# Handing out a projection's products in halves beside a windowed attention, each half bound to an attention unit's scores or to another unit's output

## The chip, the core and the metric

The kernel runs on one core of a Trainium2 chip, all in float32, with products of two parts each (below). The metric is the device time of one execution in microseconds (us). Times of several executions are given by their median.

## The reference, cut to what matters

```python
h = rms_norm(x, norm_mix)                     # x: 2048 tokens x 1024
z = h @ w_in                                  # q_A k_A v_A q_B k_B v_B gate_A gate_B
yA = windowed_gqa(q_A, k_A, v_A, sink)        # |t-s| <= 128, ALiBi, a sink logit per head
yB = neighborhood_attn(q_B, k_B, v_B, rpb)    # 8 x 16 places of a 32 x 64 grid
x = x + (sigmoid(gA) * (yA @ Wp_A) + sigmoid(gB) * (yB @ Wp_B)) @ W_out
x = x + relu(rms_norm(x, norm_mlp) @ W_up) ** 2 @ W_down
out = rms_norm(x, norm_final)
```

There are 8 query heads over 2 key heads in A, 8 heads in B, and 64 features per head.

## The kernel before, in words

TensorE does every product in three passes: each float32 operand is split into a high part and a rest, and the high-by-high, high-by-rest and rest-by-high products are added up in one PSUM bank (`mm3`, L203 to L205). The rest of the program is arranged so that TensorE is always given something to do.

The input projection is done for the first 1024 tokens in one stage of its own. For the other 1024 tokens (two blocks of 512, `b` 2 and 3) its products are **filler**: they are handed out while the two attentions run. One filler product is `feature_tile` (L207): 8 chunks of the 1024 features by three passes, 24 matmuls of 128x512 into one of the two banks called `mm`. When the 24 are done, ScalarE and VectorE read the bank and write the result in two parts (`z`), and SyncE sends it to memory. A column tile of 128 features is two such products. `qk_tile` (L706) and `v_tile` (L719) make them: load the weights, split them (`whl`), then product and eviction for block 2, then the same for block 3. The first 12 column tiles (24 products, 576 matmuls) belong beside attention A; gate tiles follow them beside attention B.

Attention A is 32 **units** (`attn_a`, L771), one for a key head and 128 queries. A unit has two parts, with a `yield` between them. The first makes four score products (L792, two matmuls each into one of three banks `s`); VectorE adds the bias and takes the maximum (L794), ScalarE the exponentials (L799), VectorE sum and reciprocal (L800, L801), and GpSimd the scaling (L803). The second turns the shares by TensorE, three or two times four transposes into one of two banks `pt` (L810), has ScalarE copy (L813) and VectorE subtract (L814) to get their two parts `ph` and `pl`, multiplies both with v (L815, L816, bank `av`), and adds the two halves of that bank (L821 on ScalarE, L822 on VectorE).

`drive` (L836) writes the units so that the second part of unit k comes behind the first part of unit k+2. This is done in two calls: 14 units, then 18.

The order on each engine isn't the order of the source. A scheduler sorts each engine's instructions: the attention, which is written first, goes first wherever it is ready by the scheduler's own clock, and filler, which is written behind it, is put where the attention isn't ready. What keeps filler from being used up too early is `paced` (L846): piece n of the filler may stand on TensorE only behind an instruction kept in the list `done`. Such a bond orders the queue when the program is built; on the chip nothing waits for it. Before the change `done` holds one mark per unit, the last matmul with v (L816, appended in L817), and a piece is one whole product: piece n stands behind unit n*32/24 - 3 (rounded down), the first three behind nothing.

```python
def paced(filler, pieces, total, lag):
    for n in pieces:
        at = min(n * 32 // total - lag, 31)
        with tc.issue_after(done[at]) if at >= 0 else nullcontext():
            next(filler, None)
```

In the profile's names, `mm<-hT,whl` is filler, `s<-ka,qa` scores, `pt<-ident,sa` transposes, `av<-ph,va` and `av<-pl,va` the products with v.

Of the kernel before, what the change touches and what calls it, by code (L numbers as in the profile page):

```python
# [22 lines left out]
P = 128  # L23
KC = D // P
# [10 lines left out]
O_QA, O_KA, O_VA, O_QB, O_KB, O_VB, O_GA, O_GB = 0, 512, 640, 768, 1280, 1792, 2304, 3328  # L35
# [60 lines left out]
def encoder_layer(ctx, tc, x, norm_mix, w_in, b_gate, sink, rpb, w_pa, w_pb, w_out,  # L96
                  norm_mlp, w_up, w_down, norm_final, dist_a, mask_b, out):
    nc = tc.nc
    V, A, G, PE, SY = nc.vector, nc.scalar, nc.gpsimd, nc.tensor, nc.sync
# [99 lines left out]
    def cols(w, c, n=P):  # L199
        return w[:, c : c + n]  # L200

    def mm3(ps, lh, ll, rh, rl, first, last):
        PE.matmul(ps, lh, rh, start=first, stop=False)  # L203
        PE.matmul(ps, lh, rl, start=False, stop=False)  # L204
        PE.matmul(ps, ll, rh, start=False, stop=last)  # L205
# [371 lines left out]
    for p in range(2):  # L577
        t = T(xp, [P, D], F32, "xin", 8).rearrange("p (k c) -> p k c", k=4)
# [15 lines left out]
    for k in range(KC):  # L594
        ps = zbank(*tbanks[k % 6])
# [7 lines left out]
        else:  # L603
            h, l = (t[:, kk] for t in right[3])
# [41 lines left out]
    for q in range(2, len(QUADS)):  # L646
# [10 lines left out]
        if q in (5, 6):  # L657

            b = q - 3
# [24 lines left out]
    hp = {}  # L684
# [18 lines left out]
    h_pages(2)  # L703


    def qk_tile(col, scale, tiled=False):  # L706
        raw = load_slice([(cols(w_in[0], col), KC)])
        yield
        hl = split_slice(raw, V if col == O_KA else G)
        yield  # L710
        for b in (2, 3):
            ps = psum("mm", 2)
            feature_tile(ps, hl, hp[b])
            out = qk_parts(col, b, ps, T(wp, [P, 2, BT], F32, "z", 3))
            for dst, t in out:
                SY.dma_start(dst, t)
            yield

    def v_tile(col):  # L719
        raw = load_slice([(cols(w_in[0], col), KC)])  # L720
        yield
        hl = split_slice(raw, V if col == O_VA else G)
        yield
        for b in (2, 3):
            ps = psum("mm", 2)
            feature_tile(ps, hl, hp[b])
# [12 lines left out]
    for h in range(4):  # L739
        at = slice(h * A_Q, (h + 1) * A_Q)  # L740
# [10 lines left out]
    done, began, shares = [], [], []  # L751
# [19 lines left out]
    def attn_a(g, i):  # L771
# [11 lines left out]
        ka, v = kas[g], vas[g]  # L783
# [4 lines left out]
        for u, (lo, hi) in enumerate(span):  # L788
            n = hi - lo
            ps = psum("s", 3)  # L790
            for z in range(2):
                PE.matmul(ps[:, :n], q[:, u].rearrange("p h q -> p (h q)"), ka[:, z, base + lo : base + hi],  # L792
                          start=z == 0, stop=z == 1)
            V.tensor_tensor_reduce(out=s[:, u, lo:hi], in0=ps[:, :n], in1=bias_a[g][:, lo - u * A_Q : hi - u * A_Q],  # L794
                                   scale=1.0, scalar=sink_g, op0=ALU.add, op1=ALU.max, accum_out=mx[:, u : u + 1])
# [11 lines left out]
        for c in range(c0, c1):  # L807
# [8 lines left out]
            last = PE.matmul(po, v[:, i - 1 + c, :], pl, start=False, stop=c == c1 - 1).ins  # L816
        done.append(last)  # L817
        t = T(ap_, [64, 512], F32, "ya", 2)
# [24 lines left out]
        while last and live:  # L843
            next(live.pop(0), None)

    def paced(filler, pieces, total, lag):  # L846

        for n in pieces:
            at = min(n * 32 // total - lag, 31)
            with tc.issue_after(done[at]) if at >= 0 else nullcontext():  # L850
                next(filler, None)

# [11 lines left out]
            yield  # L864


    dense = [qk_tile(O_KA, 1.0), v_tile(O_VA)]
    dense += [qk_tile(O_QA + t * P, 0.125) for t in range(4)]
    for t in range(4):
        dense.append(qk_tile(O_KB + t * P, 0.125))  # L870
        dense.append(qk_tile(O_QB + t * P, 1.0, tiled=True))
        dense.append(v_tile(O_VB + t * P))
    dense += [gate_tile(f, (2, 3)) for f in range(16)]
    for n in (0, 0, 1):
        next(dense[n])
# [2 lines left out]
    fill = chain(dense)  # L878
# [182 lines left out]

    first_y = load_y(0)
    first_load = last_dma[0]
    paced(fill, range(20, 44), 38, 4)
    s_h.close()


# [297 lines left out]
    for b in range(NB):  # L1365
# [43 lines left out]
        for t in range(4):  # L1409
# [182 lines left out]
    for n in (1, 6, 2, 7, 5, 3, 4):  # L1592
        for group in ((range(8),) if n != 4 else (range(4), range(4, 8))):
# [14 lines left out]
            last = []  # L1608
# [55 lines left out]
```

## Time and profile before

| what | value |
|---|---|
| median of 3 executions | 2606.39 us (2603.34, 2606.39, 2606.54) |
| the profiled execution's own time | 2603.09 us |
| its span, first to last instruction | 2601.3 us |
| TensorE matmuls | busy 2570.3 us (99%), 12140 of them |
| VectorE, ScalarE, GpSimd busy | 1608.5 us, 1232.9 us, 366.8 us |
| first score product of attention A starts | about 363 us |
| last product with v of attention A starts | about 645 us |

A matmul's row in the profile gives its start and how long it took from there to its end. Matmuls overlap: the next one starts before the last has ended, so a row of 0.39 us may be followed by a start 0.23 us later. "Busy" is the time in which at least one is under way. What a matmul costs the queue is read from the distance of the starts.

### The profile page before, as it was taken

How to read it: one execution, taken by the hardware profiler on the slowest of the kernel's cores; microseconds unless marked ns; L12 is line 12 of the kernel's file. 1: busy time of each engine (PE TensorE's matmuls, PEld its weight loads, DVE VectorE, ACT ScalarE, POOL GpSimd, SP SyncE). 2: the span in 40 equal slices, each digit the busy share in tenths (PEclk: the TensorE clock that was granted, in tenths of full speed). 3: DMA queues.
4: the chain of work that ended last, by engine and by line, in shares of the span. 5: the costliest groups of instructions: out<-in, count | busy, mean ns of one | idle time of the engine just before them, and what ended most of it. 6: DMA issues, size and time to landing. Idle time of an engine off the chain costs nothing.

```text
span 2601.3 us, 34630 instructions
## 1 busy us (share of the span) xinstructions
PE 2570.3 (99%) x12140; PEld 2143.2 (82%) x12140; DVE 1608.5 (62%) x2621; ACT 1232.9 (47%) x2261; POOL 366.8 (14%) x493
## 2 busy tenths in 40 slices
PE   8999999999999999999999999999999999999999
PEld 6888788788888888888888888888888888888887
DVE  8866666665544444665478667766656534554766
ACT  5334356665655555542335544644454322323454
POOL 1000124444645531000000000100000000000010
PEclk9999999999999999999999999999999999999999
DMA  5657485465976746865466665844428825444555
GB/s 186 203 154 207 135 260 160 121 170 154 244 211 180 205 137 189 270 205 160 144 195 213 232 227 202 307 167 149 155 102 314 288 97 186 146 149 167 186 191 173
DMA packets 354128, 490.40 MB, mean 189 GB/s; under 512 B 28809, under 2 KB 188809, under 8 KB 351777
## 3 DMA queue, kind: packets, MB, share of 16 engines
q1 hardware_dynamic: 346896, 471.14, 57.2%
q10 hardware_dynamic: 7056, 17.04, 1.8%
q8 instruction: 96, 1.57, 0.3%
q14 instruction: 80, 0.65, 0.1%
HBM read 328.64 MB, written 159.45 MB: 188 GB/s over the span
## 4 chain that ended last, share of the span: by engine, by line
PE 92%; DVE 3%; DMA 2%; ACT 2%; issue 1%; SPq 0%; POOL 0%; POOLq 0%; ACTq 0%; DVEq 0%
PE b L302 16%; PE b L304 16%; PE b L303 16%; PE mm L203 6%; PE mm L205 6%; PE mm L204 6%; PE zb L302 3%; PE zb L304 3%; PE zb L303 3%; PE pt L203 2%; PE pt L204 2%; PE pt L205 2%; PE av L995 2%; PE pt L983 2%; PE s L955 2%; PE pt L810 1%
## 5 line engine op out<-in xcount | busy, mean ns | idle before, releaser
L303 PE MATMUL b<-dwh,dah 128*128 128x512 f32 x896 | 348.5, 389 | 0.0
L304 PE MATMUL b<-dwh,dah 128*128 128x512 f32 x896 | 347.6, 389 | 0.0
L302 PE MATMUL b<-dwh,dah 128*128 128x512 f32 x896 | 339.6, 389 | 0.0
L298 ACT CAST dah<-da 128x1024 fp32r<-128x1024 f32 (+1 forms) x128 | 120.9, 945 | 367.9 <-PE b L304 245.4
L299 DVE TENSOR_TENSOR dah<-da,dah 128x1024 fp32r<-128x1024 f32 (+1 forms) x128 | 139.7, 1091 | 224.5 <-ACT dah L298 221.3
L303 PE MATMUL b<-ubh,uwhlb 128*128 128x512 f32 x592 | 230.3, 389 | 0.0
L302 PE MATMUL b<-ubh,uwhlb 128*128 128x512 f32 x592 | 230.2, 389 | 0.0
L304 PE MATMUL b<-ubh,uwhlb 128*128 128x512 f32 x592 | 229.2, 389 | 0.0
L203 PE MATMUL mm<-hT,whl 128*128 128x512 f32 x544 | 218.6, 402 | 0.0
L205 PE MATMUL mm<-hT,whl 128*128 128x512 f32 x544 | 215.3, 396 | 0.0
L204 PE MATMUL mm<-hT,whl 128*128 128x512 f32 x544 | 214.4, 394 | 0.0
L303 PEld LDWEIGHTS b<-dwh,dah 128*128 128x128 f32 x896 | 168.2, 188 | 35.0
L302 PEld LDWEIGHTS b<-dwh,dah 128*128 128x128 f32 x896 | 168.2, 188 | 34.9
L304 PEld LDWEIGHTS b<-dwh,dah 128*128 128x128 f32 x896 | 168.2, 188 | 34.9
L302 PE MATMUL zb<-zh,zwhl 128*128 128x512 f32 x476 | 186.0, 393 | 6.9 <-DVE st L242 2.0
L303 PE MATMUL zb<-zh,zwhl 128*128 128x512 f32 x476 | 185.8, 390 | 0.0
L304 PE MATMUL zb<-zh,zwhl 128*128 128x512 f32 x476 | 183.0, 390 | 1.8 <-DVE zwhl L299 1.8
L293 DVE TENSOR_TENSOR uc<-b,uc 128x512 f32<-128x512 f32 x160 | 109.2, 689 | 103.9 <-PE b L304 103.0
L1534 POOL TENSOR_TENSOR st<-st,power 128x1 f32<-128x1 f32 x16 | 13.3, 841 | 925.1 <-DVE st L1533 925.0
L302 PEld LDWEIGHTS b<-ubh,uwhlb 128*128 128x128 f32 x592 | 111.1, 188 | 23.5 <-issue 0.4
L303 PEld LDWEIGHTS b<-ubh,uwhlb 128*128 128x128 f32 x592 | 111.1, 188 | 23.1
L304 PEld LDWEIGHTS b<-ubh,uwhlb 128*128 128x128 f32 x592 | 111.1, 188 | 23.0
(255 smaller groups left out, 5842.2 us busy)
## 6 DMA issues: line engine op xcount, KB each, us to landing
at<-uc SPq DMA_DIRECT2D x224, 256.0 KB
da<-at SPq DMA_DIRECT2D x96, 512.0 KB
dw<-in_w_down_dram SPq DMA_DIRECT2D x160, 256.0 KB
uraw<-in_w_up_dram SPq DMA_DIRECT2D x32, 1024.0 KB
raw<-in_w_in_dram SPq DMA_DIRECT2D x34, 512.0 KB
zraw<-in_w_in_dram SPq DMA_DIRECT2D x16, 1024.0 KB
z<-zg SPq DMA_DIRECT2D x64, 256.0 KB
zg<-zc SPq DMA_DIRECT2D x32, 256.0 KB
```

The source lines that it names most:

```text
L203: PE.matmul(ps, lh, rh, start=first, stop=False)
L204: PE.matmul(ps, lh, rl, start=False, stop=False)
L205: PE.matmul(ps, ll, rh, start=False, stop=last)
L293: return eng.tensor_tensor(out=out, in0=a, in1=b, op=op).ins
L298: casts.append(A.copy(hi, src).ins)
L299: return eng.tensor_tensor(out=lo, in0=src, in1=hi.bitcast(F32), op=ALU.subtract).ins
L302: PE.matmul(ps, lh, rh, start=first, stop=False, skip_group_check=True)
L303: PE.matmul(ps, lh, rl, start=False, stop=False, skip_group_check=True)
L304: PE.matmul(ps, ll, rh, start=False, stop=last, skip_group_check=True)
L955: PE.matmul(ps[:, :n], q[:, i, :], kv[:, z, B_R0[i] // 4 : (B_R0[i] + B_NR[i]) // 4, 4 * B_C0[j] : 4 * (B_C0[j] + w)], start=z == 0, stop= ...
L983: PE.transpose(pt[:kp, at + (i - i0) * P : at + (i - i0 + 1) * P], s[i][:, rr : rr + kp], ident)
L995: last = PE.matmul(po[:, i0 * P : (i0 + ni) * P], v[:kp, c, :], src[:kp, o : o + ni * P], start=first, stop=(c == 7 and z == 1), skip_grou ...
```

## The change

It cuts each of the first 24 filler products in two halves of 12 matmuls (`product`, 4 of the 8 chunks each, one bank for both), so that there are 48 pieces. Every unit now appends two marks to `done`: the last score product of its first part, and as before the last product with v. With the order of `drive`, the list runs S0 S1 S2 A0 S3 A1 S4 A2 and so on to 64 marks (S: scores, A: with v). Half n stands behind mark n*64/48 - 6, the first five behind nothing. So the two halves of one product are mostly bound to different units: those of product 6 (counted from 0) are bound to S6 and A4, those of product 7 to S7 and S8. Attention B's calls get 32 as the new argument, which is the number they used before; gate tiles stay whole. The number, shape and buffers of all instructions are the same as before on every engine; only their order changes. The first instruction that stands elsewhere on TensorE is in the first units of attention A, the last one is a score product of attention B that starts at about 779 us in the profile before.

```diff
-    def feature_tile(ps, hl, pages):
+    def feature_tile(ps, hl, pages, ks=range(KC)):
         hi, lo = pages
-        for k in range(KC):
+        for k in ks:
             mm3(ps, hl[:, 0, k, :], hl[:, 1, k, :], hi[k // 4][:, k % 4, :], lo[k // 4][:, k % 4, :],
                 k == 0, k == KC - 1)
...
+    def product(ps, hl, pages, fine):
+        if fine:
+            feature_tile(ps, hl, pages, range(KC // 2))
+            yield
+        feature_tile(ps, hl, pages, range(KC // 2 if fine else 0, KC))
+
-    def qk_tile(col, scale, tiled=False):
+    def qk_tile(col, fine=False):
...
             ps = psum("mm", 2)
-            feature_tile(ps, hl, hp[b])
+            yield from product(ps, hl, hp[b], fine)
...
             for z in range(2):
-                PE.matmul(ps[:, :n], ...)
+                last = PE.matmul(ps[:, :n], ...).ins
...
+        done.append(last)
         A.activation(nm, mx, AF.Copy, scale=-1.0)
...
-    def paced(filler, pieces, total, lag):
+    def paced(filler, pieces, total, marks, lag):
         for n in pieces:
-            at = min(n * 32 // total - lag, 31)
+            at = min(n * marks // total - lag, marks - 1)
...
+    dense = [tile_of(col, n < 12) for n, (tile_of, col) in enumerate(order)]
...
-    paced(fill, range(12), 24, 3)
+    paced(fill, range(24), 48, 64, 6)
...
-    paced(fill, range(12, 24), 24, 3)
+    paced(fill, range(24, 48), 48, 64, 6)
...
-    paced(fill, range(20), 38, 4)
+    paced(fill, range(20), 38, 32, 4)
```

The first place is TensorE's queue at the first units of attention A. Before, the products of the fourth filler bank (`mm_4044`) come only behind 78 matmuls that are not filler; these rows are from the first half of them.

```order
L414 MATMUL mm_4035<-ident,z_4033 128x128 x4
L792 MATMUL s_3185<-ka_292_2963,qa_3169 128x288 x2
L815 MATMUL av_3142<-ph_3148,va_294_2965 128x512
L792 MATMUL s_3244<-ka_292_2963,qa_3240 128x288 x2
L792 MATMUL s_3248<-ka_292_2963,qa_3240 128x288 x2
L816 MATMUL av_3142<-pl_3149,va_294_2965 128x512
L815 MATMUL av_3142<-ph_3159,va_294_2965 128x512
L810 MATMUL pt_3202<-ident,sa_2967 128x128 x2
L792 MATMUL s_3252<-ka_292_2963,qa_3240 128x288 x2
```

No filler stands between these rows. Now the first half of `mm_4044`, 12 matmuls, stands in front of `s_3185`, and its second half (`hT_3015`, `hT_3016`) begins a few rows on. These are the rows from the end of the first half.

```order
L205 MATMUL mm_4044<-hT_3001,whl_3029 128x512
L798 MATMUL s_3185<-ka_292_2963,qa_3169 128x288 x2
L822 MATMUL av_3142<-ph_3148,va_294_2965 128x512
L798 MATMUL s_3244<-ka_292_2963,qa_3240 128x288 x2
L798 MATMUL s_3248<-ka_292_2963,qa_3240 128x288 x2
L823 MATMUL av_3142<-pl_3149,va_294_2965 128x512
L822 MATMUL av_3142<-ph_3159,va_294_2965 128x512
L817 MATMUL pt_3202<-ident,sa_2967 128x128 x3
L823 MATMUL av_3142<-pl_3160,va_294_2965 128x512
L817 MATMUL pt_3213<-ident,sa_2967 128x128 x3
L203 MATMUL mm_4044<-hT_3015,whl_3029 128x512
```

The stretch without filler is cut there from 78 matmuls to 24 and shorter ones.

The second place is TensorE's queue at unit 4, where products 6 (`mm_4150`) and 7 (`mm_4180`) are handed out. Before, product 6 is one row of 24 matmuls. Now its second half, which is bound to the last product with v of unit 4 (the row that reads `pl_3443`), stands behind both the first half and part of the second half of product 7, which are bound to scores of units 7 and 8.

```order
L203 MATMUL mm_4180<-hT_3015,whl_4082 128x512
L204 MATMUL mm_4180<-hT_3016,whl_4082 128x512
L823 MATMUL av_3414<-pl_3432,va_294_2965 128x512
L822 MATMUL av_3414<-ph_3442,va_294_2965 128x512
L817 MATMUL pt_3489<-ident,sa_2967 128x128 x3
L823 MATMUL av_3414<-pl_3443,va_294_2965 128x512
L817 MATMUL pt_3489<-ident,sa_2967 128x128
L817 MATMUL pt_3500<-ident,sa_2967 128x128 x4
L798 MATMUL s_3606<-ka_291_2962,qa_3598 128x288 x2
L203 MATMUL mm_4150<-hT_2935,whl_4082 128x512
L798 MATMUL s_3610<-ka_291_2962,qa_3598 128x288 x2
L204 MATMUL mm_4150<-hT_2936,whl_4082 128x512
```

So both banks end within 7 matmuls of each other, and 52 matmuls of attention follow without filler.

The third place is VectorE's queue at the start of that stretch. Before, such a stretch starts with one eviction (`z_4140`) and reads the scores as they come.

```order
L449 TENSOR_SCALAR z_4140<-mm_4115,z_4140 128x512
L794 ISA sa_2966,sta_3530<-s_3543,biasa_366_3452,byhead_2949 128x288
L794 ISA sta_3530 128x1
L814 TENSOR_TENSOR pl_3495<-pt_3489,ph_3494 128x512
L822 TENSOR_TENSOR ya_3448<-av_3414,ya_3448 64x512
L794 ISA sa_2967,sta_3601<-s_3602,biasa_366_3452,byhead_2949 128x288
```

Now two evictions stand in front of three score banks that TensorE filled before the two products ended.

```order
L449 TENSOR_SCALAR z_4175<-mm_4150,z_4175 128x512
L449 TENSOR_SCALAR z_4205<-mm_4180,z_4205 128x512
L800 ISA sa_2967,sta_3601<-s_3602,biasa_366_3452,byhead_2949 128x288
L800 ISA sta_3601 128x1
L800 ISA sa_2967,sta_3601<-s_3606,biasa_366_3452,byhead_2949 128x288
L800 ISA sa_2967,sta_3601<-s_3610,biasa_366_3452,byhead_2949 128x288
```

The three score reads moved behind the end of both filler products, and the bank that the next score product (`s_3614`) needs comes free behind the first of them.

More of the change, by code (lines that the diff above doesn't have):

```diff
@@ L717, in qk_tile, with v_tile @@
             yield
-    def v_tile(col):
+    def v_tile(col, fine=False):
         raw = load_slice([(cols(w_in[0], col), KC)])
@@ L725, in v_tile @@
             ps = psum("mm", 2)
-            feature_tile(ps, hl, hp[b])
+            yield from product(ps, hl, hp[b], fine)
             vt = T(wp, [P, 2, BT], F32, "z", 3)[:, 0]
@@ L791, in attn_a @@
             for z in range(2):
-                PE.matmul(ps[:, :n], q[:, u].rearrange("p h q -> p (h q)"), ka[:, z, base + lo : base + hi],
-                          start=z == 0, stop=z == 1)
+                last = PE.matmul(ps[:, :n], q[:, u].rearrange("p h q -> p (h q)"), ka[:, z, base + lo : base + hi],
+                                 start=z == 0, stop=z == 1).ins
             V.tensor_tensor_reduce(out=s[:, u, lo:hi], in0=ps[:, :n], in1=bias_a[g][:, lo - u * A_Q : hi - u * A_Q],
                                    scale=1.0, scalar=sink_g, op0=ALU.add, op1=ALU.max, accum_out=mx[:, u : u + 1])
+        done.append(last)
         A.activation(nm, mx, AF.Copy, scale=-1.0)
@@ L864, in gate_tile @@
             yield
-    dense = [qk_tile(O_KA, 1.0), v_tile(O_VA)]
-    dense += [qk_tile(O_QA + t * P, 0.125) for t in range(4)]
+    order = [(qk_tile, O_KA), (v_tile, O_VA)] + [(qk_tile, O_QA + t * P) for t in range(4)]
     for t in range(4):
-        dense.append(qk_tile(O_KB + t * P, 0.125))
-        dense.append(qk_tile(O_QB + t * P, 1.0, tiled=True))
-        dense.append(v_tile(O_VB + t * P))
+        order += [(qk_tile, O_KB + t * P), (qk_tile, O_QB + t * P), (v_tile, O_VB + t * P)]
+    dense = [tile_of(col, n < 12) for n, (tile_of, col) in enumerate(order)]
     dense += [gate_tile(f, (2, 3)) for f in range(16)]
@@ L1063, in encoder_layer @@
     first_load = last_dma[0]
-    paced(fill, range(20, 44), 38, 4)
+    paced(fill, range(20, 44), 38, 32, 4)
     s_h.close()
```

## The prediction

> **What bounds the kernel now.** I read the page first, then the stretch of attention A by windows, then its waits, then its start times.
>
> ```profile
> span 2601.3 us, 34630 instructions
> PE 2570.3 (99%) x12140; PEld 2143.2 (82%) x12140; DVE 1608.5 (62%) x2621; ACT 1232.9 (47%) x2261; POOL 366.8 (14%) x493
> ...
> PE 92%; DVE 3%; DMA 2%; ACT 2%; issue 1%; SPq 0%; POOL 0%; POOLq 0%; ACTq 0%; DVEq 0%
> ```
>
> TensorE is the bound, in the busy row and in the chain that ended last. The change takes no matmul away, so it can only give back time that TensorE loses between matmuls in the part whose order moves.
>
> ```profile
> core 0: us, PE busy (x) PEld busy (x) DVE busy (x) ACT busy (x) POOL busy (x), PEclk, DMA share, GB/s
> 355.00:640.00 285.00, 279.40 (x1500) 232.82 (x1499) 172.28 (x491) 183.52 (x508) 130.04 (x225) 1.00 0.60 164
> 378.20:391.50 13.30, 12.55 (x79) 10.19 (x78) 11.80 (x45) 13.25 (x48) 7.19 (x14) 1.00 0.82 252
> 417.10:424.80 7.70, 7.20 (x45) 5.78 (x44) 6.43 (x18) 7.47 (x22) 4.88 (x6) 1.00 0.62 164
> 479.90:491.30 11.40, 9.31 (x58) 7.44 (x57) 8.58 (x26) 8.01 (x21) 5.74 (x8) 1.00 0.51 134
> 517.10:524.60 7.50, 7.05 (x46) 5.66 (x45) 5.76 (x18) 6.64 (x22) 2.56 (x5) 1.00 0.64 164
> 550.60:558.80 8.20, 7.57 (x49) 6.06 (x47) 6.27 (x18) 8.10 (x23) 4.65 (x6) 1.00 0.47 129
> 583.90:591.10 7.20, 6.83 (x40) 5.25 (x39) 5.10 (x16) 6.58 (x23) 5.61 (x8) 1.00 0.81 242
> 397.20:400.80 3.60, 3.60 (x28) 3.28 (x27) 2.87 (x10) 3.28 (x7) 2.87 (x4) 1.00 0.00 0
> 451.70:456.70 5.00, 4.37 (x28) 3.50 (x27) 4.65 (x14) 5.00 (x19) 2.45 (x5) 1.00 0.33 85
> 663.30:667.40 4.10, 4.10 (x34) 3.97 (x32) 2.60 (x12) 4.01 (x13) 3.34 (x3) 1.00 1.12 338
> ```
>
> The first row is attention A with its filler: busy 279.40 of 285.00 us. The six after it are all the stretches of 40 matmuls or more in which no filler stands (78, 45, 58, 45, 49 and 40 matmuls; the counts take in one or two at the edges). Two stretches of 28 follow, then one of 32 in attention B. ScalarE is nearly full in the first (13.25 of 13.30 us). No row here shows a clock under 1.00.
>
> By the busy column, 5.60 us could be won. Start times say more.
>
> ```profile
> 477.57 0.39 PE L205 MATMUL mm<-hT,whl 128*128 128x512 f32 x1
> 477.79 0.39 PE L203 MATMUL mm<-hT,whl 128*128 128x512 f32 x1
> ...
> 484.65 0.40 PE L816 MATMUL av<-pl,va 128*128 128x512 f32 x1
> 484.89 0.60 PE L810 MATMUL pt<-ident,sa 128*128 128x128 f32 x4
> 487.51 0.66 PE L810 MATMUL pt<-ident,sa 128*128 128x128 f32 x4 [2.02 <-DVE pl L814]
> 488.11 0.50 PE L815 MATMUL av<-ph,va 128*128 128x512 f32 x1
> 488.44 0.40 PE L816 MATMUL av<-pl,va 128*128 128x512 f32 x1
> 488.68 0.39 PE L815 MATMUL av<-ph,va 128*128 128x512 f32 x1
> 488.91 0.39 PE L816 MATMUL av<-pl,va 128*128 128x512 f32 x1
> ...
> 489.81 0.95 PE L792 MATMUL s<-ka,qa 128*128 128x288 f32 x6
> 490.64 0.50 PE L816 MATMUL av<-pl,va 128*128 128x512 f32 x1
> 490.98 0.60 PE L810 MATMUL pt<-ident,sa 128*128 128x128 f32 x4
> 491.34 0.48 PE L203 MATMUL mm<-hT,whl 128*128 128x512 f32 x1
> 491.65 0.40 PE L204 MATMUL mm<-hT,whl 128*128 128x512 f32 x1
> ```
>
> Filler starts every 0.22 to 0.23 us though a row lasts 0.39. Four transposes take 0.36 us of the queue (490.98 to 491.34), two scores about 0.27 (six in 0.83), a product with v 0.23, the first one behind transposes or a wait 0.31 to 0.34. So a stretch has a cost without waits: 0.135 per score matmul, 0.36 per four transposes, 0.23 per product with v. For 479.90 to 491.30 that is 18 scores 2.43 + 28 transposes 2.52 + 12 products 2.76 = 7.7 us; it took 11.4, so 3.7 us are lost. In the same way, with counts from the same rows of start times: 378.2 has 36 scores, 28 transposes, 4 more for `v_tile` and 10 products, 10.0, lost 3.3; 417.1 has 16, 20 and 9, 6.0, lost 1.7; 517.1 lost 1.5; 550.6 (four transposes more) 1.8; 583.9 (16, 16, 8) 1.8. Those six lose **13.8 us**. The stretch at 397.2 (6 scores, 16 transposes, 6 products) loses nothing, that at 451.7 (10, 12, 6) 1.2.
>
> [...]
>
> **Why a long stretch loses.** The longest wait is the one in the rows above, and this is ScalarE before it.
>
> ```profile
> 484.09 0.52 ACT L799 ACTIVATE sa<-sa,sta 128x288 f32<-128x288 f32 x1
> ...
> 486.17 0.56 ACT L813 CAST ph<-pt 128x512 fp32r<-128x512 f32 x1
> ```
>
> ```profile
> 480.67 0.69 DVE L449 SCALAR_TENSOR_TENSOR z<-mm,z 128x512 fp32r<-128x512 f32 x1 [2.65 <-ACT z L448]
> 481.28 0.51 DVE L794 CUSTOM_DVE_ANT_0 sa<-s,biasa,byhead 128x288 f32<-128x288 f32 x1
> ...
> 481.76 0.52 DVE L794 CUSTOM_DVE_ANT_0 sa<-s,biasa,byhead 128x288 f32<-128x288 f32 x1
> ...
> 482.64 0.69 DVE L814 TENSOR_TENSOR pl<-pt,ph 128x512 fp32r<-128x512 f32 x1
> 483.24 0.51 DVE L794 CUSTOM_DVE_ANT_0 sa<-s,biasa,byhead 128x288 f32<-128x288 f32 x1
> ```
>
> The copy of `pt` stood behind four exponentials, 484.09 to 486.17, and TensorE behind the copy. And VectorE cannot keep up for long: a score read takes 0.48 us of its queue (481.28 to 481.76), a subtraction 0.60 (482.64 to 483.24), so one unit needs 4 x 0.48 + 3 x 0.60 + one sum of two halves (0.6, taken like a subtraction) = 4.3 us, while TensorE without filler does a unit in 8 x 0.135 + 3 x 0.36 + 6 x 0.23 = 3.5. Filler between is what lets VectorE catch up.
>
> **The change part by part.** The marks are bonds in the queue, no waits on the chip; nothing is added that waits, and nothing queues behind one.
>
> *The first burst.* Its 78 matmuls are cut to 24 and pieces of at most 18. Such short pieces lose between nothing (397.2) and 1.2 us per 28 (451.7); nearer to the first, since filler follows at once, I take 0.5 for all of it: 0.5 - 3.3 = **-2.8 us** (bounds -3.3 to 0).
>
> *The other long stretches.* The bonds don't even out the filler: the last product with v of unit 4 stands behind the scores of units 7 and 8, so half 13 comes after halves 14 and 15. Both `mm` banks are then open, end together, and two units run without filler. The new order has six such stretches in attention A (52, 44, 48, 56, 46, 56 = 302 matmuls) in place of five (45, 58, 45, 49, 40 = 237), which lose 10.5 us or 44 ns per matmul. 302 x 44 ns = 13.3: **+2.8 us**. Bounds by the rows: 33 ns (517.1) gives 10.0, 64 ns (479.9) gives 19.3, so -0.5 to +8.8.
>
> *Two evictions in front.* At three of the six (products 6 and 7, 12 and 13, 18 and 19) two evictions stand next to each other on VectorE ahead of score reads, where one stood. Each holds VectorE 0.6 us (480.67 to 481.28): 0 to +1.8, and **+0.5** as much of it is in the rate above.
>
> *Attention B.* The order shifts up to about 779 us: two stretches of 57 and 43 matmuls, where the longest was 32. By the row at 663.3, which is of this kind (TensorE busy throughout, 4.10 of 4.10), nothing; by 44 ns, 4.4: **+1.0**, nearer to its own kind.
>
> *Stretches of 20 to 39.* 354 matmuls become 274. At 0 to 43 ns (397.2, 451.7) the 80 less are 0 to -3.4: **-0.8**.
>
> *Switches.* Between transposes and other matmuls there are 134 changes each way before, 130 now. The first matmul behind transposes takes 0.31 us where 0.23 is usual: 4 x 0.08 = **-0.3**. [...]
>
> *At nothing:* evictions, weight splits and transfers are the same in number. TensorE hides them.
>
> ```profile
> PE pt L810 <- DVE pl L814: 2.3, 2, 2.0
> PE av L816 <- DVE pl L814: 1.4, 5, 0.4
> PE s L792 <- DVE sta L794: 0.5, 2, 0.3
> ```
>
> These are TensorE's waits between 355 and 645 us, all but 0.5 us of them: no transfer and no weight split among them. In the new order, too, product 7, say, is done before the scores of unit 10, and unit 15 is the first to read it. If that cover went, a weight tile late by a microsecond would cost that microsecond.
>
> **Sum:** -2.8 + 2.8 + 0.5 + 1.0 - 0.8 - 0.3 = **+0.4 us**. On the profiled execution's own 2603.09 (span 2601.3 and 1.8 around it) that is 2603.5; on the median 2606.39 it is 2606.8. The median lies 3.3 over the profiled one, so I take the middle, **2605 us**: no change. What a measurement can tell from no change is about 0.2%, 5.2 us.
>
> **The rivals.** *A: the halves do level the filler.* The loss of long stretches falls to that at 397.2, near nothing, because each follows closely on others and VectorE has caught up. For it: the cut of the first burst, and the stretch at 397.2, which follows another by a few us and loses nothing. Against: three score reads pending at the start of a stretch, and five stretches out of five that lost 33 ns or more. Long stretches at 10 ns lose 3.0 in place of 13.3, 10.3 less: about **2595 us**. It decides from about 25 ns per matmul on.
>
> *B: ScalarE's exponentials get in front of the copies in each long stretch,* as at 484.09. One of five stretches shows it, at 64 ns. If all 402 matmuls of the eight long stretches (302 and 57 and 43) lose that, 25.7 us in place of 14.3 + 0.5: +10.9, about **2616 us**. It decides from three stretches more that have a 2 us wait. For it: ScalarE is as full as VectorE in the rows above, and the new order keeps three runs of exponentials in the stretch of 52 matmuls; against: two of those are broken by copies or come after them.
>
> *C: the change does not do what it says.* Halves that end up next to each other are whole products. The new order has 10 filler stretches of 20 or more, before 7. Then the time stays, **2605 us**, for another reason.
>
> **How the numbers follow.** Forecast 0.45, C 0.17, both within 0.2%; A 0.17, faster; B 0.21, slower. The forecast's own bounds, with one uncertain term at a time at its end, run from 2602 to 2611. The range reaches half way into A and B: 2597 to 2614 leaves out under 0.1 on each side.
>
> **What would show it.** Right: the burst near 378 us is gone and gave some 3 us; six stretches of 44 to 56 matmuls last about 9 us each, 2.2 over their cost; the time between 378 and 779 us is the same within 2 us. Wrong for the stretches: one of 52 takes 7.5 us (A) or 10.5 with a wait of 2 us under it (B). Wrong altogether: TensorE waits for a transfer or a weight split there, or anything behind 785 us differs.

## The result, and the profile after

The changed kernel takes **2610.0 us** (median of 22 executions), the one before 2604.9 us beside it on the same chip (22 executions): a ratio of 1.0022, 95% interval 1.0016 to 1.0028, some 5 us slower. The prediction had 2605.0 and no change. The profiled execution took 2609.85 us, against 2603.09 before.

The page's head and the chain that ended last:

```profile
span 2608.1 us, 34622 instructions
...
PE 2573.9 (99%) x12140; PEld 2147.2 (82%) x12140; DVE 1605.8 (62%) x2621; ACT 1233.2 (47%) x2261; POOL 366.4 (14%) x493
...
PE 90%; DVE 4%; DMA 2%; ACT 1%; issue 1%; SPq 0%; POOL 0%; POOLq 0%; DVEq 0%; ACTq 0%
```

TensorE is still the bound, with the same 12140 matmuls. Its busy time grew by 3.6 us with no matmul added: some of them ran slower.

Since the count is the same, the place where the time went can be found by position: the start of the nth matmul in one trace against the start of the nth in the other. Up to position 1531 and from 3815 on both programs have the same order.

| positions | before | after | difference |
|---|---|---|---|
| 0 to 1531, same order | 352.5 us | 350.9 us | -1.6 |
| 1531 to 3034, attention A with filler | 285.7 us | 287.3 us | +1.6 |
| 3034 to 3815, the hand-over to attention B and on to about 779 us | 134.8 us | 139.8 us | **+5.1** |
| 3815 to the last matmul, same order | 1815.0 us | 1816.2 us | +1.2 |

The first and the last row show by how much two executions of one order differ (the first row's stretch, whose order no kernel here changes, takes 349.9 to 353.4 us in the eighteen profiled executions); only the third row is beyond that. Equal positions don't hold equal work, though. By position 3034 the kernel after has done 21 matmuls of filler more and 21 of attention fewer (11 transposes, 10 products with v), which at the prediction's prices is 1.4 of the 1.6 us in the second row, and the third row has as much less to do. Attention A came out near the forecast. These are the windows of it that answer to those of before (in each row: length, then busy time of PE, PEld, DVE, ACT, POOL, granted clock, DMA share, GB/s):

```profile
355.00:640.00 285.00, 278.88 (x1490) 232.88 (x1489) 166.25 (x486) 179.15 (x501) 129.89 (x212) 1.00 0.61 166
378.20:391.50 13.30, 13.30 (x79) 11.37 (x78) 10.50 (x37) 11.65 (x38) 8.66 (x17) 1.00 0.78 233
427.40:436.90 9.50, 9.06 (x51) 6.88 (x50) 7.95 (x25) 7.65 (x22) 4.42 (x5) 1.00 0.73 205
460.90:470.10 9.20, 7.61 (x44) 5.88 (x43) 5.83 (x17) 6.08 (x17) 5.53 (x7) 1.00 0.79 215
495.00:504.00 9.00, 8.38 (x47) 6.37 (x46) 7.10 (x18) 8.59 (x24) 4.52 (x6) 1.00 0.62 163
528.10:537.80 9.70, 8.80 (x55) 7.27 (x54) 8.01 (x25) 9.04 (x27) 5.50 (x7) 1.00 0.64 157
562.40:571.90 9.50, 7.92 (x45) 6.11 (x44) 8.03 (x23) 7.61 (x18) 3.55 (x3) 1.00 0.56 135
596.10:605.90 9.80, 9.00 (x55) 7.32 (x54) 8.15 (x25) 9.17 (x27) 4.91 (x6) 1.00 0.59 149
```

The second row is the old first burst: TensorE is now busy in all of it. The six below are the new long stretches without filler, 9.0 to 9.8 us each.

The longest of TensorE's waits from 355 to 800 us (engine, what it writes, line, whom it waited for: us in total, times, longest):

```profile
PE av L822 <- DVE ya L829: 2.7, 4, 1.4
PE s L798 <- DVE sta L800: 2.5, 4, 1.4
PE s L960 <- DMA qb<-qs_b: 2.2, 1, 2.2
PE av L1000 <- DVE ya L829: 0.6, 1, 0.6
```

The third row is a wait for a transfer, a kind that before had none of. TensorE's timeline has its place:

```profile
654.54 0.48 PE L823 MATMUL av<-pl,va 128*128 128x512 f32 x1
654.86 1.36 PE L988 MATMUL pt<-ident,sb 128*96 128x128 f32 x8
656.79 0.39 PE L1000 MATMUL av<-phb,vb 96*128 96x256 f32 x1 [0.57 <-DVE ya L829]
...
659.87 2.71 PE L960 MATMUL s<-kb,qb 128*128 128x384 f32 x6 [2.24 <-DMA qb<-qs_b]
662.38 0.41 PE L1000 MATMUL av<-plb,vb 96*128 96x256 f32 x1
662.59 0.41 PE L1000 MATMUL av<-phb,vb 96*128 96x256 f32 x1
```

At 654.54 stands attention A's last product with v. Behind it TensorE has little left that is ready: transposes and a few products of B's first unit. Then the scores of B's third unit wait for their q, and from there on the matmuls are slow: products of 256 columns start 0.21 us apart (662.38, 662.59), where two of them at 674.20 and 674.32 are 0.12 apart. The windows say why, by the granted clock in the third column from the end:

```profile
657.00:661.00 4.00, 1.76 (x8) 1.56 (x8) 0.94 (x2) 0.11 (x1) 1.89 (x2) 0.69 0.83 253
661.00:665.00 4.00, 4.00 (x17) 3.55 (x17) 2.35 (x7) 0.47 (x1) 1.94 (x2) 0.50 0.77 270
665.00:669.00 4.00, 4.00 (x24) 3.61 (x23) 2.29 (x8) 2.93 (x9) 0.00 (x0) 0.95 1.05 229
```

The clock is at half for 6.8 us, from 658.55, within the wait, to 665.38. In busy time this looks like work (4.00 of 4.00 us), which is how a busy TensorE hides a loss.

The load that was late, in SyncE's timeline of the kernel after:

```profile
654.05 0.62 SPq L922 DMA_DIRECT2D braw<-tab  x1
655.05 0.57 SPq L947 DMA_DIRECT2D qb<-qs_b  x1
```

It is issued 0.5 us behind A's last product with v, and that is no chance: the buffer `qb2` of attention B lies over one of A's buffers for `pl` (that of the `braw` in the row above over one for `ph`), and its first load waits until TensorE has read it for the last time. From issue to the first score it took 4.8 us. Before, the same three steps looked like this, first on TensorE, then on SyncE:

```profile
644.77 0.39 PE L816 MATMUL av<-pl,va 128*128 128x512 f32 x1
...
651.32 1.44 PE L955 MATMUL s<-kb,qb 128*128 128x384 f32 x6
```

```profile
645.68 0.58 SPq L942 DMA_DIRECT2D qb<-qs_b  x1
```

From issue to scores there were 5.6 us, so the transfer was hidden with 0.8 us to spare at most (in one run below the same load took 5.6 us and was waited for). What stood on TensorE in that time is the difference: 35 matmuls between A's last product with v and B's third unit before, which fill the 6.6 us there; 13 after, 2.5 us of work, and the rest of the 5.3 us is waits. The new marks hand filler out earlier. When A's last product with v comes, 29.0 filler products are done in place of 27.1, and the first gate products are not there any more to cover the load.

### The profile page after: what moved, and what is told of

It reads as the page before. It is cut to its first block, busy times and chain, and to the rows that moved or that the text cites. A ratio compares the mean times of both kernels' runs of the same rounds, so it can differ in the third digit from the quotient of the medians.

```text
span 2608.1 us, 34622 instructions
## 1 busy us (share of the span) xinstructions
PE 2573.9 (99%) x12140; PEld 2147.2 (82%) x12140; DVE 1605.8 (62%) x2621; ACT 1233.2 (47%) x2261; POOL 366.4 (14%) x493
## 4 chain that ended last, share of the span: by engine, by line
PE 90%; DVE 4%; DMA 2%; ACT 1%; issue 1%; SPq 0%; POOL 0%; POOLq 0%; DVEq 0%; ACTq 0%
PE b L302 15%; PE b L304 15%; PE b L303 15%; PE mm L203 6%; PE mm L205 6%; PE mm L204 6%; PE zb L302 3%; PE zb L304 3%; PE zb L303 3%; PE av L1000 2%; PE pt L203 2%; PE pt L204 2%; PE pt L205 2%; PE s L960 2%; PE pt L988 2%; PE pt L817 1%
## 5 line engine op out<-in xcount | busy, mean ns | idle before, releaser
L302 PEld LDWEIGHTS b<-ubh,uwhlb 128*128 128x128 f32 x592 | 111.1, 188 | 23.4 <-issue 0.4
```

Source lines behind the costliest of these rows:

```text
L302: PE.matmul(ps, lh, rh, start=first, stop=False, skip_group_check=True)
```

## The experiments

**Theory 1** after the result: the time is lost at the hand-over, where loads into space that A's last unit leaves come late, and at the half clock that follows; attention A's long stretches cost what they did before, some 44 to 52 ns per matmul, and come out even. **Rivals**: the halves themselves cost (two open banks, evictions side by side), or the new long stretches at the hand-over (57 and 43 matmuls) do, whatever is loaded there.

One thing needs no run: with halves, but with each half bound to the mark that its whole product had before, the program has exactly the order of before on TensorE. The halves move nothing by themselves; the new marks do.

All times below are medians beside runs of the kernel before on the same chip, with the ratio to it and its 95% interval.

### Gate pieces bound behind attention A (e_tail)

```diff
-            with tc.issue_after(done[at]) if at >= 0 else nullcontext():
+            behind = done[at] if at >= 0 else tail if marks == 32 and n > 1 else None
+            with tc.issue_after(behind) if behind else nullcontext():
...
+    tail = done[-1]
```

> The changed kernel, with the gate pieces 2 to 4 (which are bound to nothing) bound to the last product with v of attention A. The six long stretches in attention A stay as they are (52, 44, 48, 56, 46, 56 matmuls); only what follows them moves: 34 matmuls (6.4 us of queue by the rows' prices) stand between A's last product and the scores of B's third unit, where the changed kernel has 14 (1.9 us) and the kernel before 36 (6.9 us). Theory 1 (the 5 us come from one place: B's third unit waits for its q, whose buffer A's last unit frees, TensorE is idle 2.2 us and its granted clock falls to a half for 6.8 us): no wait of TensorE for that load, no clock under 1.00 near 660 us, time within 0.1% of before (2603 to 2607). Theory 2 (the long stretches and their evictions are slower than before): the clock stays, but the time stays 3 us or more over before (2608 or more).

Measured: 2606.5 us, 1.0004 (0.9996 to 1.0013). On TensorE and on SyncE:

```profile
643.18 0.39 PE L823 MATMUL av<-pl,va 128*128 128x512 f32 x1
...
649.46 1.45 PE L962 MATMUL s<-kb,qb 128*128 128x384 f32 x6
```

```profile
644.09 0.57 SPq L949 DMA_DIRECT2D qb<-qs_b  x1
```

The load has 5.4 us again and nobody waits for it; the six scores take 1.45 us, not 2.71. The clock stays at 1.00 there. 3.5 of the 5.1 us are back, and what is left can't be told from nothing. The bond has a price as well: in front of A's last product now stands a stretch of 47 matmuls without filler that takes 10.5 us, 4.0 more than its cost by the prediction's prices.

### The buffer of q, moved (e_early_q)

```diff
-    ap_ = pools(s_a, "left", ("ka1", "va1", "qraw", "qa", "sta", "sa", "ya", "ph", "pl", "biasa1", "byhead"), "a")
+    ap_ = pools(s_a, "left", ("ka1", "va1", "sta", "sa", "ya", "ph", "pl", "biasa1", "byhead", "qraw", "qa"), "a")
```

> The changed kernel with attention A's left buffers in another order, so that B's third q buffer lies over A's q buffers, which are free after A's last scores, and no longer over what A's last products use. TensorE's queue in A is the same, the tail has as much filler ahead of it as in the changed kernel. Theory 1: that q is loaded some 20 us earlier, the wait for it and the half clock are gone, time within 0.15% of before (2602 to 2608), if no other load takes its place (the v loads of B now stand behind A's last buffers). Theory 2: 2608 or more with no wait for a load.

Measured: 2611.2 us, 1.0024 (1.0015 to 1.0034): nothing gained. TensorE's timeline has the reason:

```profile
677.73 0.55 PE L960 MATMUL s<-kb,qb 128*128 128x288 f32 x2 [2.23 <-DMA kb<-ks_b]
```

The q is there, and now the k of B's second head is late by as much: its buffer takes in the space of `ya`, as it did before this edit, and its load waited 3.9 us for a store of `ya`. The expectation was missed because it took one load for the only one.

### One more step of lag (e_lag7, e_lag7_tail)

```diff
-    paced(fill, range(24), 48, 64, 6)
+    paced(fill, range(24), 48, 64, 7)
...
-    paced(fill, range(24, 48), 48, 64, 6)
+    paced(fill, range(24, 48), 48, 64, 7)
```

With lag 7 each half is bound to the other kind of mark, and no stretch of 40 matmuls without filler is left in attention A.

> The changed kernel with lag 7 in place of 6: the same bonds one mark later, so that halves bound to scores are now bound to products with v and the other way round. In the new order no stretch of 40 matmuls without filler is left inside attention A, and 25 matmuls (3.4 us) stand between A's last product and B's third unit. Theory 1: long stretches do lose what their rows show (15.7 us in the changed kernel), so attention A gains about 8 us, and the load is late by 1 to 2 us with or without a half clock: 2598 to 2603. Theory 2: A gains as much and no wait is left: 2597. If long stretches only gather waits that come anyway, A gains under 3 us and the time is 2604 or more.

> Lag 7 and the bound gate pieces together: no long stretch inside A, 34 matmuls ahead of B's third unit. Theory 1: both gains, no wait for a load, clock 1.00: 2595 to 2598, 0.3 to 0.4% under before. Theory 2: the same as with lag 7 alone within 2 us. If the waits come anyway: as before, 2604.

Measured: lag 7 alone 2602.7 us, 0.9992 (0.9983 to 1.0001), still with a wait of 3.1 us for `qb`, whose load was issued 5.6 us before the scores; lag 7 with the bond of e_tail **2596.5 us, 0.9965 (0.9953 to 0.9978)**, the fastest of all and faster than both kernels. Its head and hand-over:

```profile
span 2594.2 us, 34628 instructions
```

```profile
636.00:640.00 4.00, 4.00 (x23) 3.34 (x22) 1.25 (x3) 0.58 (x1) 1.91 (x2) 1.00 0.62 125
640.00:644.00 4.00, 4.00 (x26) 3.58 (x25) 2.97 (x9) 1.53 (x3) 2.00 (x2) 1.00 1.01 324
644.00:648.00 4.00, 4.00 (x24) 3.37 (x23) 2.21 (x9) 3.87 (x11) 0.61 (x2) 1.00 0.95 201
648.00:652.00 4.00, 4.00 (x22) 3.40 (x21) 2.99 (x9) 2.67 (x8) 2.69 (x4) 1.00 1.08 290
```

TensorE is busy all through, at full clock. The four kernels make a table of two by two: the lag gives 7.3 us without the bond and 9.9 with it, the bond 3.5 at lag 6 and 6.1 at lag 7. Both together give 13.5 us, more than the 10.9 of the two by themselves, so stretches and hand-over are two costs and not one.

### The bond in the kernel before (e_before_tail)

The edit of e_tail in the kernel before.

> The kernel before, with its gate pieces 2 to 4 bound to attention A's last product with v. Theory 1 (late loads at the hand-over): the kernel before has 35 matmuls (6.9 us) between that product and the scores of B's third unit and waits for no transfer there, so the bond has nothing to win: within 0.1% of before, 2602 to 2607 us, and positions 3034 to 3815 stay at 134.8 us within 1. Rival (keeping filler for attention B is worth something in itself, so that the gain of the bond says nothing of loads): as much as in the changed kernel, 3.5 us less, about 2601.

Measured: 2610.2 us, 1.0023 (1.0014 to 1.0032). Both were wrong: the bond costs 6.0 us there. On TensorE, and the window behind it:

```profile
639.00 0.50 PE L815 MATMUL av<-ph,va 128*128 128x512 f32 x1 [1.85 <-DVE ya L822]
639.34 0.50 PE L816 MATMUL av<-pl,va 128*128 128x512 f32 x1
639.63 0.63 PE L815 MATMUL av<-ph,va 128*128 128x512 f32 x1
640.06 0.63 PE L816 MATMUL av<-pl,va 128*128 128x512 f32 x1
```

```profile
640.00:644.00 4.00, 4.00 (x15) 3.16 (x14) 1.40 (x3) 1.17 (x2) 0.07 (x1) 0.64 0.69 164
```

Filler kept back for behind A is missing in front of A's end: A's last products with v wait 1.85 us for the sum of the two halves of the bank that they need, and half clock follows for 3.4 us (starts 0.43 us apart where 0.23 is usual). That is 1.85 us and half of 3.4; the rest of the 6.0 us isn't placed (the profiled execution, 2607.0 us, is the fastest of the eleven). So the bond is a trade, good only where what it uncovers is cheaper than what it covers.

### Marks without halves (e_marks)

```diff
-    dense = [tile_of(col, n < 12) for n, (tile_of, col) in enumerate(order)]
+    dense = [tile_of(col, False) for n, (tile_of, col) in enumerate(order)]
...
-    paced(fill, range(24), 48, 64, 6)
+    paced(fill, range(12), 24, 64, 6)
...
-    paced(fill, range(24, 48), 48, 64, 6)
+    paced(fill, range(12, 24), 24, 64, 6)
```

> The changed kernel with whole filler products, each bound by both kinds of marks (12 pieces of 24 per call, lag 6): the marks without the halves. Theory 1 with long stretches at about 50 ns per matmul: seven stretches of 40 to 56 matmuls in attention A (352 matmuls, after has 302), so 2.5 us more there; 24 matmuls (3.4 us) at the hand-over where after has 13 (1.9 us), so the wait for the transfer is 0 to 2 us shorter: 2609 to 2613 us, with a wait for qb of 0.5 to 2 us. Rival (cutting a product in two is what costs, by two open banks and evictions side by side): as before, 2603 to 2606.

Measured: 2611.8 us, 1.0031 (1.0019 to 1.0042), with a wait of 2.8 us for `qb`. The time is in theory 1's range; the wait is longer than the 0.5 to 2 us that it expected, though 24 matmuls stood in front of it. The halves as the culprit fall: whole products with these marks are as slow.

### Whole products at lag 7 with the bond (e_whole7_tail), and lag 9 (e_lag9_tail)

The edit of e_marks in e_lag7_tail; and 9 for 7 in e_lag7_tail.

> Whole filler products, both kinds of marks, lag 7, gate pieces 2 to 4 bound to A's last product with v: the fastest kernel so far (2596.5) without the halves. Its attention A has four stretches of 40 or more (188 matmuls), the one with halves none; at the hand-over 33 matmuls and 6.4 us in both, with a stretch of 53 there in place of 43. Theory 1 (long stretches in A cost; from lag 6 to lag 7 with the bond, 9.9 us for 302 matmuls, 33 ns each): 188 x 33 ns = 6.2, so about 2602.7, 2600 to 2605. Rival (lag and bond do it, halves are worth nothing): 2596 to 2598.

> Halves, lag 9 and the bond for gate pieces 2 to 4. No stretch of 40 or more in attention A, as with lag 7; at the hand-over one of 73 matmuls where lag 7 has 43. Theory 1: 30 matmuls at 33 to 50 ns more, 1.0 to 1.5 us: about 2598, 2596 to 2600, no wait for a transfer. Rival (handing filler out still earlier goes on helping, stretches or not): 2590 to 2594.

Measured: whole products 2606.4 us, 1.0009 (1.0000 to 1.0018); lag 9 2601.7 us, 0.9991 (0.9983 to 1.0000). At lag 7 the halves are worth 9.8 us. By the prediction's prices the four long stretches of whole products lose 8.9 us, 47 ns per matmul, more than the 33 expected and near the 52 of the kernel after; besides, the stretch of 53 in front of A's last product loses 5.3 where that of 43 loses 2.9. Lag 9 lost 5.2 us to its one stretch of 73 in front of the hand-over, three times what was expected: TensorE waits 2.0 us for `ya` in it, and the clock is at half for 6.8 us.

### Another buffer for B's third unit (e_own_q, e_before_own_q, e_lag7_own_q, e_lag7_own_q_tail)

```diff
-        q = T(bp, [P, 4, P], F32R, f"qb{n_u % 3}", 1)
+        q = T(bp, [P, 4, P], F32R, f"qb{(0, 1, 0, 2, 1)[n_u if n_u < 2 else 2 + (n_u - 2) % 3]}", 1)
```

> The changed kernel; attention B's third unit loads its q into the buffer that B's first unit has left, and the fourth into the one that lies over A's buffers (qb0, qb1, qb0, qb2, qb1, qb0 and so on in place of qb0, qb1, qb2 in turn). TensorE's order is the same up to the last units of A; the load that comes late has its first reader 9.3 us (56 matmuls) behind A's last product with v in place of 1.9. Theory 1 (late load and the half clock after it): no wait for qb, no half clock near 660 us, positions 3034 to 3815 at 134 to 136 us: 3.5 to 5 us less than after, 2605 to 2607. Rival (the long stretches at the hand-over, 57 and 43 matmuls, cost the time whatever is loaded): a stretch of 47 is left there, so at most 2 us less, 2608 to 2610.

> The kernel before with the same choice of buffers for q. Theory 1: it waits for no transfer there, so there is nothing to win, 2603 to 2606 us. Rival (the choice is worth something by itself, by scores of B's third unit that stand earlier): as much less as in the changed kernel, 2600 to 2602.

> Halves, lag 7, the choice of buffers for q, no bond for the gate pieces. Theory 1: lag 7 alone gave 2602.7 with a wait of 3.1 us for qb and half clock behind it; with both gone 4 to 6 us less, 2596.5 to 2599, as with the bond (2596.5). Rival (what the bond gave at lag 7 was the filler that it keeps, not the load): 2601 to 2604.

> Halves, lag 7, the choice of buffers for q and the bond for gate pieces 2 to 4. Theory 1: the late load is already off the path by either of the two, so both give no more than one: 2596 to 2598. Rival (the bond has a price of its own, as in the kernel before, where it cost 6.0 us by a wait of 1.9 us for the sum of the two halves and 3.4 us of half clock): slower by 2 us or more than lag 7 with the buffers alone.

Measured: 2610.3 us, 1.0025 (1.0015 to 1.0036); 2607.1, 1.0012 (1.0003 to 1.0021); 2601.4, 0.9989 (0.9980 to 0.9998); 2600.5, 0.9993 (0.9984 to 1.0001). All four missed what theory 1 expected, and e_lag7_own_q lies where its rival had put it, e_own_q at the edge of that. The traces show other late loads there, though. In e_own_q GpSimd, VectorE and TensorE read, in this order:

```profile
663.81 3.86 POOL L928 TENSOR_TENSOR biasl<-braw,masks 128x384 f32<-128x384 f32 x3 [9.04 <-DMA braw<-tab]
```

```profile
665.03 0.56 DVE L965 CUSTOM_DVE_ANT_0 sb<-s,biasl 128x384 f32<-128x384 f32 x1 [1.95 <-POOL biasl L928]
```

```profile
665.65 0.62 PE L960 MATMUL s<-kb,qb 128*128 128x384 f32 x2 [1.45 <-DVE stb L965]
```

No q is late, but the raw bias is: it too lies over A's space, GpSimd makes the bias from it, VectorE adds that to the scores, and TensorE waits for a score bank. At lag 7 the same edit leaves a wait of 2.2 us for a score bank, and with the bond one of 1.5 us for `kb`; in the kernel before it creates one of 2.6 us for `kb`.

### The buffers laid out anew (e_free_all, e_lag7_free_all, e_free_mem, e_lag7_free_mem)

The order of the pools, in which they lie in memory; for e_free_mem:

```diff
-("ka1", "va1", "qraw", "qa", "sta", "sa", "ya", "ph", "pl", "biasa1", "byhead")
+("ka1", "va1", "ya", "sa", "ph", "pl", "sta", "byhead", "biasa1", "qraw", "qa")
...
-"qb1", "qb2", "biasl", "braw1", "kb1")
+"qb1", "qb2", "braw1", "biasl", "kb1")
...
-("sb0", "sb1", "sb2", "vb0", "vb1", "vb2", "phb", "plb", "yb")
+("sb0", "sb1", "sb2", "yb", "vb2", "vb0", "vb1", "phb", "plb")
```

e_free_all has `"ya", "ph", "pl", "sta", "byhead", "biasa1", "sa", "qraw", "qa"` behind `"va1"`, and `"sb0", "sb1", "yb", "phb", "plb", "sb2", "vb2", "vb0", "vb1"`.

> The changed kernel with the buffers laid out anew: q and the raw bias of attention B lie over A's qa and qraw, the k of the second head over A's sa, the left side of B so that only yb, phb, plb and sb2 lie over what A's last unit uses. The three loads have no release by A's last product with v in front of them any more. The order of TensorE at the hand-over still has long stretches (61 and 40 matmuls; after has 57 and 43), and attention A one more of 40. Theory 1 (late loads): no wait of 1 us or more for a load or the bias made of it, no half clock there, positions 3034 to 3200 at 29 to 31 us (after 33.9, before 28.6); the time 2606 to 2609, as the stretch of 40 more costs up to 2 us. Rival (the stretches cost it): 33 us or more for these positions, 2610 to 2613.

> The same layout with lag 7 (no stretch of 40 or more in A, the hand-over with 58 and 40). Theory 1: 2597 to 2600 us, positions 3034 to 3200 at 29 to 31 us (lag 7 alone: 33.2, and 2602.7 us). Rival (stretches): 33 us or more, 2602 to 2605.

> The changed kernel with its buffers laid out so that q and the raw bias of attention B lie over qa and qraw of A, k of B's second head over ph and pl, phb and plb over sa, yb and one of the three v over ya. TensorE at the hand-over has stretches of 61 and 36 matmuls (after 57 and 43), and B's fifth unit, the first to read that k, begins 16 us behind A's last product with v. Theory 1 (what of B lies over what A's last unit uses): no wait of 1 us or more for a load, positions 3034 to 3200 at 29 to 31 us (after 33.9, before 28.6); the time 2606 to 2609, with up to 2 us for one more stretch of 40 in A. Rival (the stretches): 33 us or more, 2610 to 2613.

> The same layout with lag 7, which has no stretch of 40 or more in A and one of 53 at the hand-over. Theory 1: 2597 to 2600 us, positions 3034 to 3200 at 29 to 31 us. Rival: 33 us or more, 2602 to 2605.

Measured: 2623.8 us, 1.0067 (1.0054 to 1.0080); 2616.2, 1.0039 (1.0025 to 1.0052); 2616.3, 1.0050 (1.0036 to 1.0064); 2601.4, 0.9991 (0.9983 to 1.0000). The first two put B's `plb` over `ya`, which the expectation had not reckoned with, and VectorE's timeline of e_free_all shows the price, with a window behind it:

```profile
677.15 0.69 DVE L994 TENSOR_TENSOR plb<-pt,phb 96x512 fp32r<-96x512 f32 x1 [10.86 <-DMA y_a<-ya]
```

```profile
668.00:684.00 16.00, 7.48 (x26) 6.46 (x27) 4.37 (x12) 4.45 (x12) 4.95 (x5) 0.50 1.06 239
```

A wait of 10.86 us for a store, and TensorE for 16 us at half clock and busy less than half of the time. e_free_mem waits 2.9 us for a `kb` of a later unit and 2.4 us for `plb`. Only e_lag7_free_mem came near what was expected: 30.5 us for the hand-over, 1.4 us over the time foreseen.

By time these layouts are misses. Together they settle the rival's "whatever is loaded there", though. The stretches at the hand-over are nearly the same in after (57 and 43) and e_free_all (61 and 40), and the second takes 10.9 us longer between positions 3034 and 3200; e_lag7_free_mem has one of 53 there and is 1.9 us over before, with a wait of 1.6. Here are those positions for all kernels (from about 645 to 674 us before), with TensorE's waits in them and the time at half clock. The instructions aren't quite the same in all, which is worth a microsecond or so.

| kernel | 3034 to 3200 | over before | waits of TensorE | half clock | waits + half of it |
|---|---|---|---|---|---|
| before | 28.6 us | 0 | 0 | 0 | 0 |
| e_tail, e_lag7_tail, e_whole7_tail, e_lag9_tail | 28.8 to 29.0 | 0.2 to 0.4 | 0 | 0 | 0 |
| e_lag7_free_mem | 30.5 | 1.9 | 1.6 `stb` | 0 | 1.6 |
| e_before_tail | 30.9 | 2.3 | 1.0 `kb`, `qb` | 0 | 1.0 |
| e_lag7_own_q | 31.2 | 2.6 | 2.2 `stb` | 0 | 2.2 |
| e_own_q | 31.8 | 3.2 | 1.4 `stb` | 3.4 | 3.1 |
| e_lag7_own_q_tail | 32.2 | 3.6 | 2.2 `kb`, `stb` | 0 | 2.2 |
| e_marks | 33.0 | 4.4 | 2.8 `qb` | 3.4 | 4.5 |
| e_lag7 | 33.2 | 4.6 | 3.1 `qb` | 3.4 | 4.8 |
| e_early_q | 33.3 | 4.7 | 3.3 `kb`, `plb` | 0 | 3.3 |
| e_before_own_q | 33.9 | 5.3 | 2.6 `kb` | 3.4 | 4.3 |
| **after** | **33.9** | **5.3** | 2.8 `qb`, `ya` | 6.8 | 6.2 |
| e_free_mem | 37.7 | 9.1 | 5.3 `kb`, `plb` | 10.2 | 10.4 |
| e_lag7_free_all | 41.9 | 13.3 | 10.1 `plb`, `kb` | 13.7 | 16.9 |
| e_free_all | 44.8 | 16.2 | 12.3 `plb`, `kb`, `vb` | 17.1 | 20.8 |

At half clock TensorE's starts lie about twice as far apart (0.43 us for 0.23 in e_before_tail, 0.21 for 0.12 in after), so half of that time is taken as lost. Waits, and half of the time at half clock, account for what the hand-over takes over before within 1.5 us up to 9 us (above that the two overlap). Kernels without a wait there are at 28.6 to 29.0 us. That says nothing of stretches: the four with the bond have theirs (43 to 73 matmuls) in front of A's last product, ahead of position 3034, where they lose 2.9 to 8.8 us by the prediction's prices.

## Why the prediction was wrong, step by step

- **The first burst** (-2.8 us): right. Its stretch of 78 is gone, and the 24 matmuls left of it lose 0.65 us by the same prices, where 0.5 was taken.
- **The other long stretches** (+2.8, and +0.5 for the two evictions): right in kind, a little small. There are six, of 9.0 to 9.8 us. By the prediction's prices they lose 2.5, 3.1, 2.3, 2.3, 3.3 and 2.4, together 15.7 us over 302 matmuls, 52 ns each where 44 and the evictions made 13.8. None has a wait of 2 us, so rival B is not what made the kernel slower, and rival A's level filler did not come either.
- **All of attention A**: by those prices (filler at 0.227 us) it lost 23.2 us before and 23.4 after, positions 1620 to 3034. The forecast of about nothing was right there. No run separates the two small terms (-0.8 and -0.3).
- **Rival C** (halves next to each other are whole products): the order did move, but at this lag the halves changed little, as e_marks shows with whole products, 7.6 us over before beside 5.1.
- **Attention B** (+1.0 us): measured +5.1 from position 3034 to 3815. The stretch of 57 was priced by its matmuls alone. As there is 1.4 us less to do at these positions, the loss is nearer 6.5.
- **The step that failed** is "At nothing: evictions, weight splits and transfers are the same in number. TensorE hides them." It was argued from the waits of before between 355 and 645 us, and from filler's own weights. It did not look at which loads are released by A's last product with v, nor how much work TensorE had behind that product. In before's trace a load of `qb` started 645.68 and was used at 651.32, and the new order left 2.5 us of work there. "Same in number" was true, and said nothing on when. With a cover of 6.3 us given back (e_tail) the wait is gone and 3.5 us with it, which is the greater part of the result; in ten kernels of the table TensorE waits for a transfer by name, and the two forms of the edit that took its `qb` away (e_early_q, e_own_q) moved the wait to `kb` and to the bias made from `braw`.
- **The clock** had no term at all. The prediction read "no row here shows a clock under 1.00" and left it at that; in after a wait of 2.24 us came with 6.8 us at half clock, half of which is about 3 us more.
- **What would show it wrong altogether** was named rightly, "TensorE waits for a transfer", and is what the trace shows.

How much of it is the wait and how much the clock can be estimated. In the table it is 2.6 us over before for a wait of 2.2 at full clock, and 4.4 for one of 2.8 with 3.4 us at half clock. Over all executions the granted clock is 0.9978 on average in the 22 of after, 0.9989 in the 109 of before that stood beside the experiments and 0.9990 in the 11 of e_tail: after is at half clock for some 5.7 us more than before, which costs 2.9 of the 5.1 us, and the bond takes that away.

What stays open: the order is made anew for each layout of the buffers, so that every one that freed a load also moved others; a kernel with the order of after and no late load was not found.

## What to carry to other kernels

Where two stages share memory, the first loads of the second start when the first stage's last readers are done: list them, and measure in the trace how much ready work stands between that release and their first use (here 5.6 us for a load that takes 4.8 to 5.6). A change that hands out filler earlier spends that cover at the end, so its price stands at the next hand-over and not where the order was changed. And where pieces are bound to two kinds of marks in turn, try the lag by ones: 6 and 7 differ by 7 to 10 us here, because of which pieces fall on which mark.

## What the runs showed of the hardware

The granted clock of before is 1.00 from 16 to 2599 us. In after it is at half from 658.55 to 665.38 us, 6.83 us. Of the experiments, e_before_tail shows it at half for 3.4 us and e_free_all for 17.1 us; the times of the others at the hand-over are in the table above. In the 3.41 us ahead of the fall TensorE had been idle for 1.61 us in after and for 1.99 in e_before_tail.

The length of a wait alone didn't tell here whether the clock fell. Around the wait of 2.02 us that ends at 487.51 in the kernel before, which the prediction quotes, the clock stays full. These are two windows of 3.41 us there, with TensorE busy for 2.18 and 2.55 us:

```profile
483.24:486.65 3.41, 2.18 (x14) 1.63 (x13) 1.45 (x6) 2.86 (x11) 1.36 (x2) 1.00 0.81 215
486.65:490.06 3.41, 2.55 (x15) 2.11 (x16) 3.32 (x11) 2.12 (x5) 1.95 (x4) 1.00 0.66 170
```

In e_before_own_q, whose order is the same up to there, the same wait (2.03 us) lies in the first of the next two windows, where TensorE is busy for 1.38 us, and the second is at half clock:

```profile
484.36:487.77 3.41, 1.38 (x10) 0.96 (x9) 1.94 (x5) 3.11 (x10) 1.51 (x4) 1.00 0.85 230
487.77:491.18 3.41, 3.41 (x12) 2.81 (x12) 2.23 (x8) 1.02 (x2) 0.44 (x1) 0.50 0.21 42
```

Behind the wait of 2.2 us in e_lag7_own_q the clock stayed full (1.00 in all windows from 650 to 674 us); in after it fell within one of 2.24 us. What decides it is not shown. Before and e_before_own_q have one order up to their wait, so there the half clock is a difference between two executions and not between two orders.
